# TensorE's order written out by hand in the prompt attention of a hybrid decoder trunk, and the token gates in two passes instead of three

## Chip, cores and metric

One core of one Trainium2 chip runs the whole step. The metric is the device time of one execution in microseconds. Three runs of the kernel before took 1816.46, 1821.41 and 1823.29 us; the median is 1821.41 us.

## What is computed

The reference is one decoder layer on 1024 prompt tokens (`x_prompt`) and 8 x 4 sample tokens (`x_sample`, at positions behind a paged cache of 2048). All is float32. Cut to what matters here:

```python
z = rms_norm(x, g_norm1) @ w_in          # u, v, q, six k/v heads, 24 token gates, 2048 merge gates
o_a = gmlp_mix(gelu(u), layer_norm(gelu(v)))          # mixer A, chunks of 128 tokens
# mixer B: per query head, three attention branches on the same tokens
o_c = softmax(q_n @ kc.T + m_c) @ vc     # compressed blocks (compress() of raw k, v)
o_s = softmax(q_r @ ks.T + m_s) @ vs     # selected blocks of 64 (prompt: 16 of 16, so all are taken)
o_w = softmax(q_r @ kw.T + m_w) @ vw     # sliding window of 512
o_b = g[0] * o_c + g[1] * o_s + g[2] * o_w            # g = sigmoid(token gates)
x = x + (sigmoid(g_a) * (o_a @ w_a) + sigmoid(g_b) * (o_b @ w_b)) @ w_out
x = x + square(relu(rms_norm(x) @ w_up)) @ w_down
```

`compress(rows, w1, w2, pe)` maps every 32 cached k (or v) rows, at a stride of 16, through a small two-layer network. It runs on the prompt's rows and on the 8 samples' caches, for k and for v.

## The kernel before

Products that need float32 precision are made of three products of rounded parts: a value is split into a high part (ScalarE copies it to float32r) and a low part (VectorE or GpSimd subtracts), and TensorE adds high x high, high x low and low x high in PSUM. The helpers are short, so their lines stand for many operations: `cp` (L54, ScalarE copy), `tt` (L57, VectorE with two tensors), `mm` (L73, TensorE matmul), `Weights.split` (L120, the low part of a weight block on VectorE or GpSimd).

The program is unrolled. It is written with a planner: each engine's instructions are ordered ahead of time by a simulated timeline, in which an instruction that comes earlier in the program text, or stands in a `high_priority` block, goes first among those that are ready. A region `tc.manual_schedule(engines={...})` takes the named engines out of the planner's hands: inside it they issue in the order of the program text. The other engines, and instructions outside the region, are still planned. At run time every engine takes its instructions strictly in the order so fixed, and waits on semaphores.

The stages, with their place in the profiled execution: projections of k, v and the token gates (to about 110 us), mixer A and the q projection (to about 233 us), **the prompt's attention** with the samples' compression and twelve merge-gate blocks (about 230 to 705 us), the samples' attention with eight more gate and u blocks (to about 895 us), branch and output projections and the MLP (to the end).

The prompt's attention takes 32 pairs (`pairs`: 8 blocks of 128 queries, each for 4 pairs of heads). A pair's key blocks (selected branch, window branch, one block of compressed keys) are cut into chunks of four blocks of 128 keys: 2 to 7 chunks a pair, 160 in all, 560 blocks. For each chunk there are three pieces:

- an A step (`a_steps`, `step`): `logits` makes the chunk's products of queries and keys on TensorE (bank tag `S`, 3 buffers; tile `P`, 8 buffers); `stat` on VectorE takes row maxima; when all of a head's branch is there, `group` has ScalarE take exponentials, `fin` on VectorE the factors, `scale` on GpSimd multiplies `P`;
- `T(c)`: TensorE transposes the chunk's four blocks of `P` into a bank `PT` (2 buffers); ScalarE copies the high part to `PH`, VectorE subtracts the low part;
- `PV(c)`: TensorE multiplies the values with both parts of `PH` into the pair's bank `O` (1 buffer).

After a pair's last `PV` follows `E`, which adds up, and stores to `o_d`. `q_trans(i)` transposes a pair's queries. In the text before, a pair's `T` runs two chunks ahead of its `PV` (`PV(c)`, then `T(c + 2)`), with A steps of the next pair between them, and the planner may move other work in between on TensorE.

The samples' compression takes 16 blocks (8 samples, k and v): 16 page loads on SP's queue (`raw`, 2 buffers), four quarter splits (`hl`, 2 buffers; ScalarE, then GpSimd or VectorE), 24 matmuls of 256 columns into the single bank `F`, then a small network (`comp_hidden`, `comp_out`, `comp_knorm`) through the same bank. The twelve gate blocks (`fillers` over `W0`) take 72 matmuls of 352 columns each into the single bank `G`; a block's weights (`wraw`, `whl`, one buffer each) are loaded on GpSimd's queue and split by ScalarE and GpSimd, and `gate_evac3` evicts. Compression and gate blocks stand behind the attention in the text, so the planner puts their TensorE work where the attention leaves room.

The token gates (`gates`) are 72 matmuls: 8 k-slices x 3 products x 3 column thirds, with 24 output rows.

Of the kernel before, what the change touches and what calls it, by code (L numbers as in the profile page):

```python
# [15 lines left out]
TB = 352  # L16
# [16 lines left out]
HPU = 2  # L33
# [3 lines left out]
LEAD = 1  # L37
# [8 lines left out]
def build(tc, a):  # L46
# [18 lines left out]
    def mul(out, x, y):  # L65
        return tt(out, x, y, OP.mult)
# [227 lines left out]
    wg = pv.tile([128, 2, 8, 24], F32R, name="wg")  # L294
# [178 lines left out]
    split(wg[:, 0], wg[:, 1], wg_r)  # L473
# [234 lines left out]
    def a_steps(u):  # L708
# [124 lines left out]
    def c_steps(u, chunks, Ps):  # L833
# [32 lines left out]
        def E():  # L866
# [9 lines left out]
            SP.dma_start(o_d[4 + pr, :, qb * 128:(qb + 1) * 128], o)  # L876
# [3 lines left out]
    hp = tc.high_priority()  # L880
    hp.__enter__()
    q_load(0)
    q_load(1)
    q_trans(0)
    prev = None
    for u in range(len(pairs) + 1):
        if u == HPU:
            hp.__exit__(None, None, None)
        A, C = [], 0
        if prev:  # L890
            pu, pch, pPs = prev
            T, PV, E = c_steps(pu, pch, pPs)
            C = len(pch)
            T(0)
            T(1)
        if u < len(pairs):
            chunks, Ps, A = a_steps(u)
            prev = (u, chunks, Ps)
            A.pop(0)()
            q_trans(u + 1)  # L900
        n_a = len(A)
        for c in range(C):
            PV(c)
            T(c + 2)
            k = min(n_a, -(-n_a * (c + LEAD) // C))
            while A and n_a - len(A) < k:
                A.pop(0)()
        while A:
            A.pop(0)()
        if C:  # L910
            E()


# [48 lines left out]
    ctxm = tc.manual_schedule(engines={mybir.EngineType.SP})  # L962
    ctxm.__enter__()
    for which in range(2):
        w1, bias, w2 = c_weights(which)
        for b in range(8):
            raw = cl()
            tg = "FG"[b % 2] if which * 8 + b < N3 else "F"
            pb = bank(tg, 1, psS)
            out = pb[:, 0:256].rearrange("p (k g r) -> p k g r", k=2, r=8)  # L970
            for qt in range(4):
                hl = pa.tile([128, 2, 16, 32], F32R, name="hl", bufs=HIB)
                cols = slice(qt * 32, (qt + 1) * 32)
                with tc.high_priority():
                    cp(hl[:, 0], raw[:, :, cols])
                    (POOL if qt else DVE).tensor_tensor(hl[:, 1], raw[:, :, cols], f(hl[:, 0]), op=OP.subtract)
                hv, lv = (hl[:, i].rearrange("p g (o k r) -> p o k g r", k=2, r=8) for i in range(2))
                for o in range(2):
                    mm(out, w1[:, 0, qt * 2 + o], hv[:, o], qt + o == 0, False)
                    mm(out, w1[:, 1, qt * 2 + o], hv[:, o], False, False)  # L980
                    mm(out, w1[:, 0, qt * 2 + o], lv[:, o], False, qt == 3 and o == 1)
            with tc.high_priority():
                g = comp_hidden(pb[:, 0:256].rearrange("p (k c) -> p k c", k=2), 128, bias, pa)
                pb2 = bank(tg, 1, psS)
                comp_out(pb2[:, 0:128], g, w2)
                if which == 0:
                    z = comp_knorm(pb2[:, 0:128], pa, gkc, 1)
                    pt = bank(tg, 1, psS)
                    PE.transpose(pt[:, 0:128], z, ident)
                    pb2 = pt  # L990
                co = small([128, 128], "co", 1, p=pa)
                cp(co, pb2[:, 0:128])
                POOL.dma_start(c_d[which, b], co)
# [10 lines left out]

    TAGS = {"S": SB, "F": FB, "G": 1}

    def fillers(W, blocks, tag):
        n = 0
        for b in blocks:
            w = W.get(FM_MG + b)  # L1010
            evac = gate_evac3 if b < 16 else u_evac
            for c in range(3):
                cs = slice(c * TB, (c + 1) * TB)
                tg = tag(n)
                n += 1
                ps = bank(tg, TAGS[tg], psS)
                for k in range(8):
                    mm(ps[:, 0:TB], w[:, 0, k], X[:, 0, k, cs], k == 0, False)
                    mm(ps[:, 0:TB], w[:, 0, k], X[:, 1, k, cs], False, False)
                    mm(ps[:, 0:TB], w[:, 1, k], X[:, 0, k, cs], False, k == 7)  # L1020
                with tc.high_priority():
                    evac(b, c, cs, ps)
            W.ahead()

    def fill(W, blocks, tag):

        for b in blocks:
            w = W.get(FM_MG + b)
            for c in range(3):
                cs = slice(c * TB, (c + 1) * TB)  # L1030
                ps = bank(tag, 1, psS)
                for k in range(8):
                    mm(ps[:, 0:TB], w[:, 0, k], X[:, 0, k, cs], k == 0, False)
                    mm(ps[:, 0:TB], w[:, 0, k], X[:, 1, k, cs], False, False)
                    mm(ps[:, 0:TB], w[:, 1, k], X[:, 0, k, cs], False, k == 7)
                with tc.high_priority():
                    (gate_evac3 if b < 16 else u_evac)(b, c, cs, ps)
                if c == 2:
                    W.ahead()
                yield  # L1040

    def gate_evac3(b, c, cs, ps):
        zt = wst0.tile([128, TB], F32, name="zt", bufs=2) if b < NF0 else fp.tile([128, TB], F32, name="yt", bufs=2)
        mul(zt, ps[:, 0:TB], rep[:, cs])
        ACT.activation(zt, zt, AF.Tanh, scale=0.5)
        (ACT if b < 8 else POOL).dma_start(th_d[b, :, cs], zt)

    def u_evac(b, c, cs, ps):
        s_ = fp.tile([128, TB], F32, name="sl", bufs=2)
        POOL.dma_start(s_, s_d[b - 16, :, cs])  # L1050
        zt = fp.tile([128, TB], F32, name="zu", bufs=2)
        mul(zt, ps[:, 0:TB], rep[:, cs])
        y = fp.tile([128, TB], F32, name="yt", bufs=2)
        ACT.activation(y, zt, AF.Square, scale=GC)
        DVE.scalar_tensor_tensor(y, y, 1.0, zt, op0=OP.add, op1=OP.mult)
# [153 lines left out]
    for G in range(2):  # L1209
# [8 lines left out]
        for c in range(5):  # L1218
# [4 lines left out]
            for _ in range(NF1):  # L1223
                next(f1, None)
# [332 lines left out]
```

## Time and profile before

| what | value |
|---|---|
| median of three runs | 1821.41 us |
| profiled execution: its time / its span | 1822.3 us / 1820.5 us |
| instructions | 30327 |
| TensorE matmul busy | 1755.1 us, 96% of the span, 11095 matmuls |
| VectorE / ScalarE / GpSimd busy | 939.4 / 701.3 / 411.3 us |
| mean granted TensorE clock | 0.985 |

The span reaches from the first to the last instruction; 1.8 us of the execution lie outside it. A matmul's busy time includes its modelled way through the array, so that matmuls overlap; what one costs in a stream is read from start to start. [...] PE is TensorE, PEld its weight loads, DVE VectorE, ACT ScalarE, POOL GpSimd, SP the queue that issues most transfers.

### The profile page before, as it was taken

To read this page: it belongs to the slowest core of one execution; us is meant where nothing else is said; L and a number is where in the kernel's file an instruction comes from. 1 tells how busy PE (TensorE), PEld (TensorE's weight loads), DVE (VectorE), ACT (ScalarE), POOL (GpSimd) and SP (SyncE) were. 2 spreads that over 40 slices of the span, in tenths; PEclk is the share of its full clock that TensorE was granted. 3 is DMA by queue.
4 is the path that set the end of the run, shared out by engine and by line. 5 is a ranking of instruction groups with operands and counts; after the bars stand their busy time and mean duration, and the time that the engine had idled before them with its cause. 6 is when DMAs were issued, how large, how long until landed. Compare 5 with 4: busy or idle time off the path is not lost.

```text
span 1820.5 us, 30327 instructions
## 1 busy us (share of the span) xinstructions
PE 1755.1 (96%) x11095; PEld 1657.1 (91%) x11095; DVE 939.4 (52%) x2371; ACT 701.3 (39%) x1681; POOL 411.3 (23%) x603
## 2 busy tenths in 40 slices
PE   8999989999999987999999999999999999999999
PEld 7877878999999975667899999999999999999999
DVE  7637867877777884125664454333333333333333
ACT  5534567777677773222422333201320122003300
POOL 3103465765556653122000220000000000000000
PEclk9999989999999997999899999999999999999999
DMA  5232454333332324666543221111111111111121
GB/s 201 93 99 64 133 152 115 110 102 95 110 95 82 84 63 136 198 195 195 167 154 111 90 75 47 47 47 47 40 43 47 47 47 47 47 47 47 47 83 60
DMA packets 157703, 168.71 MB, mean 93 GB/s; under 512 B 51825, under 2 KB 132338, under 8 KB 157554
## 3 DMA queue, kind: packets, MB, share of 16 engines
q1 hardware_dynamic: 140194, 135.77, 24.0%
q0 software_dynamic: 6464, 20.19, 3.3%
q10 hardware_dynamic: 10896, 10.82, 1.8%
q8 instruction: 87, 1.43, 0.3%
q14 instruction: 62, 0.51, 0.1%
HBM read 136.54 MB, written 29.13 MB: 91 GB/s over the span
## 4 chain that ended last, share of the span: by engine, by line
PE 83%; DVE 7%; DMA 3%; SPq 3%; issue 2%; ACT 2%; POOL 1%; ACTq 0%; DVEq 0%; POOLq 0%
PE S L73 27%; PE G L73 18%; PE PT L73 14%; PE F L73 10%; PE O L73 10%; PE PT L846 2%; SPq L934 2%; DMA ol<-o_d 1%; DVE PH L57 1%; SPq L926 1%; DVE S L776 1%; PE PT L701 1%; DMA ring<-cs 1%; DMA xr<-xT 0%; DMA kct<-c_d 0%
## 5 line engine op out<-in xcount | busy, mean ns | idle before, releaser
L73 PE MATMUL G<-big,whl 128*128 128x352 f32 x1440 | 271.1, 333 | 14.6 <-ACT whl L54 7.6
L73 PEld LDWEIGHTS G<-big,whl 128*128 128x128 f32 x1440 | 235.7, 192 | 43.0 <-issue 17.2
L54 ACT ACTIVATE whl<-wraw 128x1024 fp32r<-128x1024 f32 x100 | 106.1, 1061 | 429.8 <-PE S L73 145.4
L73 PE MATMUL S<-U,whl 128*128 128x352 f32 x864 | 201.0, 323 | 0.0
L73 PE MATMUL S<-H,whl 128*128 128x352 f32 x840 | 189.8, 323 | 0.0
L73 PE MATMUL PT<-U,whl 128*128 128x352 f32 x576 | 154.4, 323 | 0.0
L800 POOL TENSOR_SCALAR P<-P,rs 128x128 f32<-128x128 f32 (+4 forms) x272 | 132.1, 501 | 79.9 <-DVE rs L57 53.0
L73 PEld LDWEIGHTS S<-U,whl 128*128 128x128 f32 x864 | 149.8, 188 | 0.0
L73 PEld LDWEIGHTS S<-H,whl 128*128 128x128 f32 x840 | 144.7, 188 | 0.0
L73 PE MATMUL PT<-H,whl 128*128 128x352 f32 x528 | 142.8, 323 | 0.0
L785 ACT ACTIVATE P<-S,nm 128x512 f32<-128x512 f32 (+3 forms) x208 | 108.8, 532 | 23.2 <-DVE nm L57 14.9
L73 PE MATMUL S<-wt,big 128*128 128x512 f32 x408 | 104.2, 402 | 10.0 <-ACT wt L54 6.4
L57 DVE TENSOR_TENSOR PH<-PT,PH 128x512 fp32r<-128x512 f32 (+2 forms) x160 | 98.5, 618 | 29.4 <-ACT PH L54 28.8
L120 DVE TENSOR_TENSOR whl<-wraw,whl 128x1024 fp32r<-128x1024 f32 x80 | 97.8, 1222 | 15.0 <-ACT whl L54 15.0
L73 PEld LDWEIGHTS PT<-U,whl 128*128 128x128 f32 x576 | 103.2, 188 | 0.0
L73 PE MATMUL O<-PH,V 128*128 128x256 f32 x528 | 95.9, 305 | 6.8 <-DVE PH L57 6.7
L54 ACT ACTIVATE PH<-PT 128x512 fp32r<-128x512 f32 (+2 forms) x160 | 86.6, 544 | 39.0 <-PE PT L846 38.0
L73 PEld LDWEIGHTS S<-wt,big 128*128 128x128 f32 x408 | 76.1, 191 | 27.2 <-ACT wt L54 6.4
L73 PE MATMUL F<-H,whl 128*128 128x352 f32 x312 | 100.9, 323 | 0.0
L73 PE MATMUL S<-KT,QT 128*128 128x128 f32 (+3 forms) x416 | 96.5, 344 | 3.9 <-ACT P L785 2.9
L73 PE MATMUL O<-H,whl 128*128 128x352 f32 x312 | 98.8, 323 | 0.0
L846 PE MATMUL PT<-ident,P 128*128 128x128 f32 x560 | 93.0, 282 | 5.3 <-POOL P L800 3.1
(371 smaller groups left out, 3763.0 us busy)
## 6 DMA issues: line engine op xcount, KB each, us to landing
wraw<-wfm SPq DMA_DIRECT2D x80, 512.0 KB, 3.2
ring<-cs SPq DMA_DIRECT2D x128, 128.0 KB, 2.2
wraw<-wfm POOLq DMA_DIRECT2D x20, 512.0 KB, 4.4
tg<-th_d SPq DMA_DIRECT2D x48, 176.0 KB, 3.0
qdl<-qd_d SPq DMA_DIRECT2D x64, 128.0 KB, 2.8
raw<-cck SPq DMA_DIRECT2D x128, 64.0 KB, 1.9
raw<-ccv SPq DMA_DIRECT2D x128, 64.0 KB, 1.9
wtr<-wtok SPq DMA_DIRECT2D x24, 256.0 KB, 2.6
```

The source lines that it names most:

```text
L54: return ACT.activation(out, in_, AF.Copy, scale=scale)
L57: return DVE.tensor_tensor(out, x, y, op=op)
L73: return PE.matmul(out, l, r, start=start, stop=stop, skip_group_check=skip)
L120: (POOL if i < FM_BR else DVE).tensor_tensor(t[:, 1], raw, f(t[:, 0]), op=OP.subtract)
L701: PE.transpose(pt[:, j], src[:, j], ident)
L776: DVE.tensor_tensor_reduce(S, S, m, scale=-1.0, scalar=3e38, op0=OP.add, op1=OP.min, accum_out=dst)
L785: ACT.activation(Ps[c][:, lo:hi], Ss[c][:, lo:hi], AF.Exp, bias=nm[:, 0, k:k + 1], scale=todo[h, br, i], accum_out=sm[:, i, k:k + 1])
L800: POOL.tensor_scalar(P, P, rs[:, 1, k:k + 1], 1.0, op0=OP.mult, op1=OP.mult)
L846: PE.transpose(pt[:, j], Ps[c][:, j * 128:(j + 1) * 128], ident)
L926: _, vals = nc.values_load_multi_w_load_instructions(ptab[0:1, i0:i0 + 16], engines=[mybir.EngineType.SP], min_val=0, max_val=159, skip_ru ...
L934: SP.dma_start(dst, src)
```

## The change

1. **Token gates.** The high and low weight parts stand side by side in one stationary operand of 56 columns (0 to 23 and 32 to 55, the rest set to zero by GpSimd). Each of 8 k-slices takes 2 products x 3 thirds: 48 matmuls. Behind them, for each third, ScalarE copies the low rows out of PSUM and VectorE adds them to the high rows.
2. **Order by hand.** The attention, the compression and the twelve gate blocks are one `manual_schedule` region for SP and PE. The 160 chunks are steps. In step s TensorE gets, in this order: `PV` of chunk s - 7, the logits of chunk s, at a fixed rate a piece of compression (64 pieces over 166 steps) and a half third of a gate block (72 over 166, 12 matmuls each), once a pair the next queries' transposes, and `T` of chunk s - 6 (`LAG = 6`).
3. **What goes with it.** `compression` and `fill` are generators that yield between pieces; the small tiles `nm`, `sm`, `rs` get 5 buffers; the store of `o_d` moves from SP's queue to GpSimd's; the samples' attention takes twice as many, half as long filler pieces.

```diff
-    wg = pv.tile([128, 2, 8, 24], F32R, name="wg")
+    wg = pv.tile([128, 8, 56], F32R, name="wg")
...
-            for i, j in ((0, 0), (0, 1), (1, 0)):
+            for j in range(2):
                 for c in range(3):
-                    mm(pss[c][0:24, 0:TB], wg[:, i, k], X[:, j, k, c * TB:(c + 1) * TB], k + i + j == 0, k == 7 and i == 1)
+                    mm(pss[c][0:56, 0:TB], wg[:, k], X[:, j, k, c * TB:(c + 1) * TB], k + j == 0, k == 7 and j == 1)
...
-            mul(gt[:, cs], pss[c][0:24, 0:TB], rep[0:24, cs])
+            cp(gt[:, cs], pss[c][32:56, 0:TB])
+            add(gt[:, cs], pss[c][0:24, 0:TB], gt[:, cs])
+            mul(gt[:, cs], gt[:, cs], rep[0:24, cs])
...
-    split(wg[:, 0], wg[:, 1], wg_r)
+    POOL.memset(f(wg), 0.0)
+    split(wg[:, :, 0:24], wg[:, :, 32:56], wg_r)
...
-        nm = small([128, 3, 6], "nm", 3, p=p2)
-        sm = small([128, 3, 6], "sm", 3, p=p2)
-        rs = small([128, 2, 6], "rs", 3, p=p2)
+        nm = small([128, 3, 6], "nm", 5, p=p2)
+        sm = small([128, 3, 6], "sm", 5, p=p2)
+        rs = small([128, 2, 6], "rs", 5, p=p2)
...
-            SP.dma_start(o_d[4 + pr, :, qb * 128:(qb + 1) * 128], o)
+            POOL.dma_start(o_d[4 + pr, :, qb * 128:(qb + 1) * 128], o)
...
-        for c in range(C):
-            PV(c)
-            T(c + 2)
-            k = min(n_a, -(-n_a * (c + LEAD) // C))
-            while A and n_a - len(A) < k:
-                A.pop(0)()
...
-    ctxm = tc.manual_schedule(engines={mybir.EngineType.SP})
...
+    f0, comp = fill(W0, range(NF0), "G"), compression()
+
+    ctxm = tc.manual_schedule(engines={mybir.EngineType.SP, mybir.EngineType.PE})
+    ctxm.__enter__()
+    q_load(0)
+    q_load(1)
+    q_trans(0)
+    A, C, steps = {}, {}, []
+    for u, (qb, pr) in enumerate(pairs):
+        n = -(-(2 * (qb + 1 + min(qb + 1, 5)) + 1) // 4)
+        steps += [(u, c, c == n - 1) for c in range(n)]
+    nc_ = nf_ = 0
+    total = len(steps) + LAG
+    for s_ in range(total + 1):
+        if s_ > LAG:
+            u, c, last = steps[s_ - LAG - 1]
+            C[u][1](c)
+            if last:
+                C.pop(u)[2]()
+        if s_ < len(steps):
+            u, c, last = steps[s_]
+            if c == 0:
+                chunks, Ps, A[u] = a_steps(u)
+                assert len(chunks) == sum(x[0] == u for x in steps)
+                C[u] = c_steps(u, chunks, Ps)
+            A[u][c]()
+        while nc_ * total < 64 * s_:
+            next(comp, None)
+            nc_ += 1
+        while nf_ * total < 6 * NF0 * s_:
+            next(f0, None)
+            nf_ += 1
+        if s_ < len(steps) and steps[s_][1] == 0:
+            q_trans(steps[s_][0] + 1)
+        if LAG <= s_ < total:
+            u, c, last = steps[s_ - LAG]
+            C[u][0](c)
+    for g in (f0, comp):
+        for _ in g:
+            pass
+    ctxm.__exit__(None, None, None)
```

`c_steps` returns `T, PV, E`, so that `C[u][0]` is `T`, `C[u][1]` is `PV` and `C[u][2]` is `E`. `fill` yields after k-slice 3 and after each third; `compression` yields after its second quarter, after its fourth, after `comp_out` and at the block's end.

## Rows read from the trace of the kernel before

**Rows 1.** The page: busy time of TensorE, its share of the span, instructions.

```profile
PE 1755.1 (96%) x11095; PEld 1657.1 (91%) x11095; DVE 939.4 (52%) x2371; ACT 701.3 (39%) x1681; POOL 411.3 (23%) x603
```

**Rows 2.** Windows (us from the start), each engine's busy us, clock, DMA.

```profile
core 0: us, PE busy (x) PEld busy (x) DVE busy (x) ACT busy (x) POOL busy (x), PEclk, DMA share, GB/s
230.00:705.00 475.00, 443.24 (x3140) 423.28 (x3139) 362.61 (x1207) 338.50 (x1001) 282.33 (x467) 0.96 0.33 97
300.00:440.00 140.00, 140.00 (x1025) 137.31 (x1024) 107.50 (x366) 106.63 (x313) 91.77 (x144) 1.00 0.36 104
680.00:716.00 36.00, 24.95 (x151) 21.09 (x151) 20.82 (x63) 14.92 (x43) 15.72 (x22) 0.72 0.29 91
1215.00:1260.00 45.00, 45.00 (x280) 45.00 (x279) 15.01 (x27) 4.25 (x4) 0.00 (x0) 1.00 0.13 43
```

**Rows 3.** Groups by line and tile: count, busy us, mean ns, idle before.

```profile
L73 PE MATMUL S<-KT,QT 128*128 128x128 f32 (+3 forms) x416 | 96.5, 344 | 3.9 <-ACT P L785 2.9 <-DVE nm L57 0.7 <-DVE QT L57 0.3
L73 PE MATMUL O<-PH,V 128*128 128x256 f32 x528 | 95.9, 305 | 6.8 <-DVE PH L57 6.7
L846 PE MATMUL PT<-ident,P 128*128 128x128 f32 x560 | 93.0, 282 | 5.3 <-POOL P L800 3.1 <-DVE QT L57 1.8
L73 PE MATMUL F<-hl,w1s 128*128 128x256 f32 x384 | 61.5, 290 | 0.4 <-ACT co L54 0.4
L993 POOL DMA_DIRECT2D c_d<-co x16 | 9.5, 596 | 8.7 <-ACT co L54 8.7
```

**Rows 4.** TensorE's timeline in the dense part: start, us, what.

```profile
347.97 1.58 PE L73 MATMUL F<-hl,w1s 128*128 128x256 f32 x12
349.39 0.63 PE L73 MATMUL S<-KT,QT 128*128 128x512 f32 x2
349.86 0.64 PE L73 MATMUL O<-PH,V 128*128 128x256 f32 x4
350.33 0.60 PE L846 MATMUL PT<-ident,P 128*128 128x128 f32 x4
350.69 0.56 PE L73 MATMUL G<-big,whl 128*128 128x352 f32 x2
```

**Rows 5.** Timeline near the attention's end, one chunk from T to PV.

```profile
700.66 1.06 PE L846 MATMUL PT<-ident,P 128*128 128x128 f32 x4
...
701.81 0.60 ACT L54 ACTIVATE PH<-PT 128x512 fp32r<-128x512 f32 x1 [2.07 <-PE PT L846]
...
702.44 0.69 DVE L57 TENSOR_TENSOR PH<-PT,PH 128x512 fp32r<-128x512 f32 x1 [1.98 <-ACT PH L54]
...
703.19 1.22 PE L73 MATMUL O<-PH,V 128*128 128x256 f32 x4
```

**Rows 6.** Windows of 4 us around three idle times: PE busy, clock.

```profile
456.00:460.00 4.00, 2.35 (x16) 0.97 0.37 103
460.00:464.00 4.00, 4.00 (x24) 0.60 0.45 150
552.00:556.00 4.00, 2.44 (x12) 0.92 0.27 83
556.00:560.00 4.00, 4.00 (x19) 0.65 0.31 115
664.00:668.00 4.00, 2.46 (x20) 1.00 1.04 315
668.00:672.00 4.00, 3.48 (x30) 1.00 0.09 31
```

**Rows 7.** TensorE's timeline: what stood behind these idle times, in brackets.

```profile
458.27 0.33 PE L989 MATMUL F<-ident,ck_z 128*128 128x128 f32 x1 [1.28 <-DVE ck_z L470]
...
554.04 1.40 PE L73 MATMUL S<-KT,QT 128*128 128x384 f32 x6 [1.56 <-ACT P L785]
...
668.40 0.42 PE L73 MATMUL F<-kct,qp 128*32 128x128 f32 x8 [1.94 <-DMA kct<-c_d]
```

**Rows 8.** Tile hl: min, median, max ns, first and last start us.

```profile
L73 PE MATMUL F<-hl,w1s x384: 272/282/415, 266.1 to 649.2; 128*128 128x256 f32 x192
```

**Rows 9.** Tile wg, the same columns.

```profile
L73 PE MATMUL PT<-big,wg x48: 317/322/406, 93.8 to 106.1; 128*24 128x352 f32 x48
```

**Rows 10.** Tile smask (the samples' ranking), the same columns.

```profile
L1150 DVE TENSOR_SCALAR smask<-cnt x2: 169/171/173, 688.2 to 696.8; 128x30 f32<-128x30 f32 x2
```

More of the change, by code (lines that the diff above doesn't have):

```diff
@@ L36 @@
 N3 = 0
-LEAD = 1
+LAG = 6
 PB = 8
@@ L875, in E, with fill @@
                 POOL.tensor_tensor(o[64 * h:64 * h + 64], t1[0:64, h], t3[:, h], op=OP.add)
-            SP.dma_start(o_d[4 + pr, :, qb * 128:(qb + 1) * 128], o)
+            POOL.dma_start(o_d[4 + pr, :, qb * 128:(qb + 1) * 128], o)
         return T, PV, E
[L880 to L898, printed above, removed]
-            A.pop(0)()
-            q_trans(u + 1)
-        n_a = len(A)
-        for c in range(C):
-            PV(c)
-            T(c + 2)
-            k = min(n_a, -(-n_a * (c + LEAD) // C))
-            while A and n_a - len(A) < k:
[L907 to L911, printed above, removed]
+    def fill(W, blocks, tag):
+        for b in blocks:
+            w = W.get(FM_MG + b)
+            for c in range(3):
+                cs = slice(c * TB, (c + 1) * TB)
+                ps = bank(tag, 1, psS)
+                for k in range(8):
+                    mm(ps[:, 0:TB], w[:, 0, k], X[:, 0, k, cs], k == 0, False)
+                    mm(ps[:, 0:TB], w[:, 0, k], X[:, 1, k, cs], False, False)
+                    mm(ps[:, 0:TB], w[:, 1, k], X[:, 0, k, cs], False, k == 7)
+                    if k == 3:
+                        yield
+                with tc.high_priority():
+                    (gate_evac3 if b < 16 else u_evac)(b, c, cs, ps)
+                if c == 2:
+                    W.ahead()
+                yield
@@ L961, in build @@
     cl = Ahead([lambda w=w, b=b: c_load(w, b) for w in range(2) for b in range(8)], RAWA)
-    ctxm = tc.manual_schedule(engines={mybir.EngineType.SP})
-    ctxm.__enter__()
[L964 to L993, printed above, removed]
@@ new lines, in compression @@
+    def compression():
+        for which in range(2):
+            w1, bias, w2 = c_weights(which)
+            for b in range(8):
+                raw = cl()
+                pb = bank("F", 1, psS)
+                out = pb[:, 0:256].rearrange("p (k g r) -> p k g r", k=2, r=8)
+                for qt in range(4):
+                    hl = pa.tile([128, 2, 16, 32], F32R, name="hl", bufs=HIB)
+                    cols = slice(qt * 32, (qt + 1) * 32)
+                    with tc.high_priority():
+                        cp(hl[:, 0], raw[:, :, cols])
+                        (POOL if qt else DVE).tensor_tensor(hl[:, 1], raw[:, :, cols], f(hl[:, 0]), op=OP.subtract)
+                    hv, lv = (hl[:, i].rearrange("p g (o k r) -> p o k g r", k=2, r=8) for i in range(2))
+                    for o in range(2):
+                        mm(out, w1[:, 0, qt * 2 + o], hv[:, o], qt + o == 0, False)
+                        mm(out, w1[:, 1, qt * 2 + o], hv[:, o], False, False)
+                        mm(out, w1[:, 0, qt * 2 + o], lv[:, o], False, qt == 3 and o == 1)
+                    if qt == 1:
+                        yield
+                yield
+                with tc.high_priority():
+                    g = comp_hidden(pb[:, 0:256].rearrange("p (k c) -> p k c", k=2), 128, bias, pa)
+                    pb2 = bank("F", 1, psS)
+                    comp_out(pb2[:, 0:128], g, w2)
+                yield
+                with tc.high_priority():
+                    if which == 0:
+                        z = comp_knorm(pb2[:, 0:128], pa, gkc, 1)
+                        pt = bank("F", 1, psS)
+                        PE.transpose(pt[:, 0:128], z, ident)
+                        pb2 = pt
+                    co = small([128, 128], "co", 1, p=pa)
+                    cp(co, pb2[:, 0:128])
+                    POOL.dma_start(c_d[which, b], co)
+                yield
@@ L1002, in build @@
     fp = pool("fp")
[L1005 to L1055, printed above, removed]
-        ACT.activation(y, y, AF.Tanh, scale=GT)
-        DVE.scalar_tensor_tensor(y, y, 1.0, zt, op0=OP.add, op1=OP.mult)
-        DVE.scalar_tensor_tensor(y, y, 0.5, s_, op0=OP.mult, op1=OP.mult)
-        POOL.dma_start(o_d[b - 16, :, cs], y)
@@ L1061, in build @@
-    W0 = Weights(wst0, 1, range(FM_MG, FM_MG + NF0))
-    fillers(W0, range(NF0), lambda i: "G")
     ps3 = pool("ps3")
@@ L1222, in build @@
             s_logits(S, qp, G, lambda j: kv[:, :, j, 0:128])
-            for _ in range(NF1):
+            for _ in range(2 * NF1):
                 next(f1, None)
```

18 lines of the change are left out of this document (added).

## The prediction

> **What bounds the kernel now.** I read the page's busy times first. TensorE is busy for 96% of the span [rows 1], so at first sight it bounds everything. But that figure holds the matmuls' way through the array, so the next view is the windows [rows 2]. In an MLP stretch TensorE issues 280 matmuls of 352 columns in 45 us, 0.161 us each, and nothing stands between them: this is what a saturated TensorE looks like. The first 140 us of the dense part of the attention are saturated too, at clock 1.00. The stage as a whole is not: it takes 475 us, and VectorE, the next engine, is busy for 363 of them.
>
> How much TensorE work is in the stage? Counts come from the groups [rows 3] and from the code, prices from start to start in the dense part [rows 4]:
>
> - gate blocks: 12 x 72 = 864 at 0.161 = 139 us;
> - compression: 384 at (349.39 - 347.97)/12 = 0.118, 45 us, and some 40 small ones at about 0.1, 4 us;
> - `PV`: 528, and 64 on compressed keys (two a pair), at (350.33 - 349.86)/4 = 0.118, 70 us;
> - transposes: 560 of `P`, 128 of queries (four a pair), at (350.69 - 350.33)/4 = 0.09, 62 us;
> - logits: 416, and 128 on compressed keys (four a pair). 528 key blocks of 128 columns, each against two query parts, and 128 times 64 columns make 263 columns on average, between 128 (0.09) and 512 (0.235): 0.14 by width, 77 us.
>
> Together 397 us, 2.5 us a step for 160 steps. An upper bound is the mean of the dense part, 140/1025 = 0.137 us, for these 3112: 425 us, but that part holds more of the wide gate matmuls. So 475 - 397 = 78 us are lost to idle time and to a lower clock, much of it at the end, where the windows show TensorE busy for 25 of 36 us at a mean clock of 0.72. These 78 us are the most that a better order can win.
>
> **The order by hand.** The matmuls stay the same; their order and their waits change. I follow TensorE through one step: `PV(s-7)`, logits of s, a piece of compression, a half third of a gate block, `T(s-6)`. Then the next step begins, and it begins with `PV(s-6)`. Between `T` of a chunk and `PV` of the same chunk stands nothing. LAG gives the softmax six steps, but the way from the transposes through ScalarE's high part and VectorE's low part back to TensorE gets no cover at all, and TensorE cannot take anything else, since its order is fixed. The queue behind the waiting `PV` is everything: the next logits, and so VectorE's row maxima and ScalarE's exponentials; compression; gate blocks. Before, `T` ran two chunks ahead of its `PV`, with logits and other work between.
>
> The price is in the trace where nothing else is left to cover it, near the attention's end [rows 5]. The four transposes end at 701.72, ScalarE's copy takes 0.60, VectorE's subtraction 0.69, and `PV` starts at 703.19: 1.47 us. From start to start it is more: four transposes fill 0.36 us of TensorE, but end 0.60 after their start [rows 4], so the loss is 1.47 + 0.24 = 1.71 us. Of the 160 chunks 32, each pair's last, have one to three blocks and cost less; 1.6 us is my mean and my lower bound. On top comes waiting in the queues of ScalarE and VectorE: each step has on average 338/160 = 2.1 us of ScalarE work and 363/160 = 2.3 us of VectorE work [rows 2], and the exponentials of the step's own logits become ready at about the time that the transposes end. Nothing excludes a wait of one full exponential; nothing in steps with few fillers forces any. I bound it by 0 and 0.9 us and take 0.35, nearer to the lower end because both engines would be less than half busy in longer steps. So each step loses 1.95 us, and 160 steps lose 312 us.
>
> **The clock.** An idle time of 1.28 us in a dense stretch [rows 7] was followed by 4 us at a mean clock of 0.60, and one of 1.56 us by 0.65; one of 1.94 us was followed by 1.00 [rows 6]. So waits of this size often, not always, put TensorE back to half speed for a while. Here there is one every step. The nearest stretch is the attention's end: 25 of 36 us busy, clock 0.72 [rows 2]. In the new steps the fillers make longer busy runs, so I take 0.8 for the stage; the ends are 1.00 and 0.50. At 0.8 the 397 us become 496.
>
> [...]
>
> **Where the stage starts and ends.** In step 1 the first piece of compression stands in TensorE's order. Its first matmul came at 266 before [rows 8], bound by page loads that cannot begin sooner, and I keep that. Before, attention and gate matmuls ran ahead of it; now nearly all wait behind it. So the stage ends at 266 + 496 + 312 = 1074 us instead of 705: +369. The samples' ranking, ready at 697 before [rows 10] and so hidden under the attention, needs memory and the bank `F` that compression now holds to the last step; the gate fillers cover most of that chain, I add 8 us, between 0 and the 29 us from the first product on the samples' compressed keys at 668 [rows 7] to the ranking's end.
>
> **What costs nothing.** 32 stores of `o_d` move to GpSimd's queue; a like one there takes 0.596 us [rows 3], 19 us on an engine busy for 282 of 475 us, in a stage that gets longer: the cover is its own idle time. Were that gone, `P` would come later, with six steps of slack behind it. On SP only loads are left, in text order: page loads can hold up a pair's query load, which has a pair's length to spare. The larger buffers of `nm`, `sm` and `rs` are needed since six steps can span four pairs. A gate block's split (ScalarE, then GpSimd) has over two steps until the next block's first matmul, some 10 us. VectorE's work of 2.3 us a step stays below the step.
>
> **The gates.** 24 of 72 matmuls go. They stood among 12.3 us [rows 9], so at most 24 x 0.17 = 4 us; the added copies and additions lengthen a chain that q and v matmuls cover; if not covered, they could eat the gain. I take -3, between -4 and 0.
>
> **Sum.** The profiled execution took 1822.3 us with a span of 1820.5, 0.9 above the median of the three runs. 1822.3 + 369 + 8 - 3 = 2196 us. Everything behind the stage moves back unchanged.
>
> **The rivals.**
>
> - *The clock stays up* (25%). Same waits, but the idle times are too short to lower the clock: 266 + 397 + 312 = 975, +270, with the other terms 2097 us. With no queueing, 160 x 1.6 = 256 us, it is 2041. For it: the 1.94 us idle time without a fall. Against it: the two others, and a wait in every step.
> - *The clock stays down* (12%). All matmuls at half speed, 794 us, and 1.8 us a step because slower TensorE leaves emptier queues: 266 + 794 + 288 = 1348, +643, 2470 us. Against it: runs of compression and gate matmuls let it recover, as the dense part shows.
> - *Not slower* (4%). The copy and the subtraction would have to be hidden so far that a step loses under (705 - 266 - 397)/160 = 0.26 us, which decides the sign; with none the stage ends at 663 and the time is 1822.3 - 42 + 5 = 1785 us. For it: the lost 78 us exist, and gate work would be left for the end. Against it: [rows 5] alone, over six times that per step.
> - The forecast has 55%; 4% remain for a mishap that I don't see, such as queueing far above 0.9 us.
>
> **Range.** From 2050 (clock up, nearly no queueing) to 2380 (clock near 0.62: 640 us, and 2.2 us a step: 266 + 640 + 352 = 1258, +553). It holds the forecast, most of the second case and little of the third, some 8 in 10. Faster by over 0.5% (the least that tells from no change here, some 9 us): 0.04; within 0.5%: 0.01; slower: 0.95.
>
> **What the profile would show.** Right: `PV` matmuls waiting on VectorE's `PH` about 160 times, 250 to 400 us in all, where now 6.8 us stand [rows 3]; a period of 4.5 to 6 us from one logits group to the next; granted clock between 0.6 and 0.9 through the stage; gate matmuls to its very end; the stage ending near 1070; 48 gate matmuls. Wrong: if `PV` waits stay below 1 us a step, if another wait (a bank `S`, weights of a gate block, pages) is larger than that on `PH`, or if the MLP changes too.

## The result and the profile after

The changed kernel takes 2156.69 us (median of four runs, 2153.15 to 2162.02) against 1820.99 us of the kernel before on the same chip: 1.185 times as long, with a 95% interval of 1.183 to 1.187. The forecast was 2196 us with a range of 2050 to 2380. The profiled execution of the changed kernel took 2157.89 us with a span of 2156.1 us, that of before 1822.3 us.

The page of the changed kernel: first TensorE's and the other engines' busy times, then two lines of the 40 slices, then the group of the `PV` matmuls.

```profile
PE 1842.8 (85%) x11071; PEld 1715.0 (80%) x11071; DVE 969.1 (45%) x2374; ACT 717.6 (33%) x1684; POOL 428.7 (20%) x636
...
PE   8999567666666666666799899999999999999999
...
PEclk9999788889988899898899999999999999999999
...
L73 PE MATMUL O<-PH,V 128*128 128x256 f32 x528 | 105.8, 324 | 222.4 <-DVE PH L57 222.4
```

Against [rows 1] TensorE has 24 instructions fewer, is busy for 88 us longer and fills 85% of the span instead of 96%. The slices say where: from the fifth to the twentieth, 54 us each, it is busy for five to seven tenths at a granted clock of seven to nine tenths, and after that it is full as before. The `PV` group waits 222 us on VectorE's low part, where [rows 3] had 6.8.

Next the waits of TensorE over the attention stage, 255 to 1038 us: what was waited for, total us, times, the longest.

```profile
PE O L73 <- DVE PH L57: 251.5, 159, 3.6
PE F L73 <- ACT hl L54: 21.1, 1, 21.1
```

One wait has taken the stage over: 159 of the 160 chunks wait, for 251.5/159 = 1.58 us each (the 64 `PV` matmuls on compressed keys are included here, which the page's group leaves out). The second line, 21 us once, ends where the first compression matmul begins; the stage's other two waits, not shown, come to 1.3 us. The tiles of the stage's start and end, and of the ranking behind it (min, median, max ns, first and last start):

```profile
L73 PE MATMUL F<-hl,w1s x384: 272/286/581, 255.3 to 1011.6; 128*128 128x256 f32 x192
...
L73 PE MATMUL O<-PH,V2C x64: 274/386/583, 278.3 to 1037.0; 128*128 128x256 f32 x64
...
L1144 DVE TENSOR_SCALAR smask<-cnt x2: 165/173/181, 1045.0 to 1053.2; 128x30 f32<-128x30 f32 x2
```

Compression begins at 255.3, where [rows 8] had 266.1, and the last `PV` stands at 1037.0, where the kernel before had 705.2. Medians tell of the clock too: the `PV` on compressed keys has 386 ns in the middle of its 64, before it had 283. Two of them took 0.80 us at 444.06, at a granted clock of 0.50, and in the kernel before 0.40 at 342.35, at 1.00.

TensorE's timeline of two steps (start, us, what, the idle time before it in brackets):

```profile
432.19 0.60 PE L849 MATMUL PT<-ident,P 128*128 128x128 f32 x4
432.82 0.60 ACT L54 ACTIVATE PH<-PT 128x512 fp32r<-128x512 f32 x1 [0.16 <-PE PT L849]
433.45 0.69 DVE L57 TENSOR_TENSOR PH<-PT,PH 128x512 fp32r<-128x512 f32 x1 [0.42 <-ACT PH L54]
434.20 0.75 PE L73 MATMUL O<-PH,V 128*128 128x256 f32 x4 [1.41 <-DVE PH L57]
434.78 0.53 PE L73 MATMUL S<-KTC,QT 128*128 128x64 f32 x4
435.14 2.18 PE L73 MATMUL G<-big,whl 128*128 128x352 f32 x12
437.16 0.60 PE L849 MATMUL PT<-ident,P 128*128 128x128 f32 x4
437.36 1.06 ACT L54 ACTIVATE whl<-wraw 128x1024 fp32r<-128x1024 f32 x1 [0.52 <-PE G L73]
438.32 0.58 ACT L54 ACTIVATE PH<-PT 128x512 fp32r<-128x512 f32 x1
438.93 0.69 DVE L57 TENSOR_TENSOR PH<-PT,PH 128x512 fp32r<-128x512 f32 x1 [1.05 <-ACT PH L54]
439.68 0.74 PE L73 MATMUL O<-PH,V 128*128 128x256 f32 x4 [1.92 <-DVE PH L57]
```

The first step shows the bare way: transposes end at 432.79, copy and subtraction follow with 0.03 us between them, and TensorE has stood still for 1.41 us. In the second step ScalarE is still splitting a gate block's weights (`whl`, 1.06 us) when the transposes end at 437.76, so the copy begins 0.56 us behind them instead of 0.03, and TensorE waits 1.92 us. This is the queueing for which the prediction took 0.35 us a step.

### The profile page after: what moved, and what is told of

It is laid out like the page before. It is cut to its first block, busy times and chain, and to the rows that moved or that the text cites. A ratio compares the mean times of both kernels' runs of the same rounds, so it can differ in the third digit from the quotient of the medians.

```text
span 2156.1 us, 30189 instructions
## 1 busy us (share of the span) xinstructions
PE 1842.8 (85%) x11071; PEld 1715.0 (80%) x11071; DVE 969.1 (45%) x2374; ACT 717.6 (33%) x1684; POOL 428.7 (20%) x636
## 4 chain that ended last, share of the span: by engine, by line
PE 76%; DVE 9%; ACT 8%; issue 3%; SPq 2%; DMA 2%; POOL 0%; ACTq 0%; DVEq 0%; POOLq 0%
PE S L73 25%; PE G L73 17%; PE PT L73 12%; PE O L73 11%; PE F L73 9%; DVE PH L57 4%; ACT PH L54 3%; PE PT L849 2%; ACT P L788 2%; SPq L942 1%; ACT hl L54 1%; DMA ol<-o_d 1%; DVE S L779 1%; DVE QT L57 1%; SPq L934 1%
## 5 line engine op out<-in xcount | busy, mean ns | idle before, releaser
L73 PE MATMUL G<-big,whl 128*128 128x352 f32 x1440 | 291.3, 358 | 6.1 <-DVE zu L57 4.5
L73 PE MATMUL O<-PH,V 128*128 128x256 f32 x528 | 105.8, 324 | 222.4 <-DVE PH L57 222.4
L73 PEld LDWEIGHTS G<-big,whl 128*128 128x128 f32 x1440 | 267.2, 216 | 35.0 <-issue 16.5
L73 PEld LDWEIGHTS O<-PH,V 128*128 128x128 f32 x528 | 76.4, 202 | 256.2 <-DVE PH L57 256.0
L779 DVE CUSTOM_DVE_ANT_0 S<-S,mask 128x256 f32<-128x256 f32 (+3 forms) x160 | 77.1, 482 | 131.1 <-PE S L73 126.5
L73 PE MATMUL S<-wt,big 128*128 128x512 f32 x408 | 107.3, 411 | 10.6 <-ACT wt L54 6.6
```

The lines of the kernel that those rows point to most:

```text
L73: return PE.matmul(out, l, r, start=start, stop=stop, skip_group_check=skip)
L779: DVE.tensor_tensor_reduce(S, S, m, scale=-1.0, scalar=3e38, op0=OP.add, op1=OP.min, accum_out=dst)
```

## Experiments

All times stand beside runs of the kernel before on the same chip. Each edit is against the changed kernel unless another is named.

| run | median us | ratio to before, 95% |
|---|---|---|
| the change | 2156.69 | 1.185 (1.183 to 1.187) |
| e1_pv_late | 1901.73 | 1.044 (1.040 to 1.048) |
| e2_gates_only | 1820.18 | 0.9997 (0.9984 to 1.0010) |
| e3_text_planned | 1851.36 | 1.017 (1.013 to 1.020) |
| e4_fill_behind_t | 1988.18 | 1.094 (1.091 to 1.098) |
| e5_high_only | 2001.34 | 1.100 (1.096 to 1.104) |
| e6_late_start | 1905.49 | 1.047 (1.045 to 1.049) |
| e7_pv_later | 1893.71 | 1.040 (1.038 to 1.042) |
| e8_logits_first | 1893.28 | 1.040 (1.038 to 1.042) |
| e9_planned_lead | 1819.20 | 0.9989 (0.9979 to 0.9998) |
| e10_fine_pieces | 1899.40 | 1.043 (1.041 to 1.045) |
| e11_spread_planned | 1813.01 | 0.995 (0.994 to 0.997) |

**`PV` one step later (e1).** A whole step of other matmuls now stands between `T` and the `PV` of the same chunk.

```diff
-    for s_ in range(total + 1):
-        if s_ > LAG:
-            u, c, last = steps[s_ - LAG - 1]
+    for s_ in range(total + 2):
+        if s_ > LAG + 1:
+            u, c, last = steps[s_ - LAG - 2]
```

> The changed kernel with one index moved: PV of a chunk stands a whole step behind its T, with the next logits, compression and gate work between them; all else, the order by hand too, stays. Theory (the uncovered way from T to PV, and the clock that it pulls down, are the whole loss): waits of PV on PH fall from 252 us to under 25 us, the granted clock of the stage is above 0.95, the attention ends between 660 and 690 us, and the time is 1775 to 1800 us, below the kernel before. Rival (a fixed order on TensorE is what costs, whichever wait shows it): another wait of 100 us or more takes its place and the time stays above 1950 us.

It measured 1901.73 us: 255 us of the 336 are back, the rest is not. TensorE's waits over its stage:

```profile
PE F L73 <- ACT hl L54: 21.6, 1, 21.6
PE O L73 <- DVE PH L57: 20.7, 26, 3.6
PE O L73 <- DVE o_t L57: 15.5, 16, 1.5
PE PT L849 <- DVE QT L57: 5.7, 8, 2.1
PE S L73 <- ACT P L788: 5.2, 4, 1.9
PE G L73 <- POOL whl L120: 5.1, 5, 2.2
```

The wait on `PH` fell from 251.5 us in 159 times to 20.7 in 26, and others came up in its place: on `o_t`, which frees the accumulator `O`; on the transposed queries; on exponentials; on a gate block's low part. So the placement of `PV` right behind `T` is the main cause, shown by one edit, but my expectation that the kernel would then be faster than before missed by 100 us: an order by hand has a second cost.

**The gates alone (e2).** Against the kernel before: `wg` with the low part in rows 32 to 55, two passes, copy and addition behind them, and nothing else of the change.

```diff
-            for i, j in ((0, 0), (0, 1), (1, 0)):
+            for j in range(2):
...
-                    mm(pss[c][0:24, 0:TB], wg[:, i, k], X[:, j, k, c * TB:(c + 1) * TB], k + i + j == 0, k == 7 and i == 1)
+                    mm(pss[c][0:56, 0:TB], wg[:, k], X[:, j, k, c * TB:(c + 1) * TB], k + j == 0, k == 7 and j == 1)
```

> The kernel before with the token gates alone in two passes of 56 columns. Theory: 24 matmuls fewer at 0.17 us, so 1 to 4 us faster, ratio 0.998 to 1.000, with 48 matmuls on the gate weights. Rival: the three added copies and additions lengthen the chain to the sigmoid, and the time rises by 1 to 3 us.

1820.18 us over 12 runs, a ratio of 0.9997: between 3 us saved and 2 us lost. The gates' tile shows the matmuls gone:

```profile
L73 PE MATMUL PT<-big,wg x32: 317/321/405, 94.0 to 102.2; 128*56 128x352 f32 x32
```

They end 3.9 us earlier than in [rows 9], as I had counted, and in the profiled execution the attention's last `PV` is earlier too, 702.1 instead of 705.2. The medians differ by 0.9 us, and their interval holds both the 3 us that I had forecast and none: whether the gain reaches the end of the kernel is not shown.

**The changed text, TensorE's order planned (e3).** The steps, the spreading and the text's order stay; only SP's order is fixed, as it was before.

```diff
-    ctxm = tc.manual_schedule(engines={mybir.EngineType.SP, mybir.EngineType.PE})
+    ctxm = tc.manual_schedule(engines={mybir.EngineType.SP})
```

> The changed kernel's text with TensorE given back to the planner (SP alone stays by hand). Theory: the planner puts other ready work between T and PV, so PV waits on PH stay under 60 us and the time is 1790 to 1850 us. Rival (the text itself costs: LAG of 6, the finer pieces, o_d on GpSimd's queue, more buffers): the time stays above 2000 us with TensorE planned.

1851.36 us, 305 us of the 336 back. The planner moves other matmuls into the gap between `T` and `PV`; the wait that the text would cause is nearly gone:

```profile
PE O L73 <- DVE PH L57: 11.9, 19, 1.8
```

It is still 32 us slower than before. The order of the text, even where it only guides the planner, costs something too: e9 below keeps the finer pieces, the larger buffers and the stores on GpSimd's queue, has another order, and does not lose these 32 us.

**Fillers behind `T` (e4).** Query transposes and `T` go ahead of compression and gate pieces, so that in a step with a filler this covers the chain.

```diff
+        if s_ < len(steps) and steps[s_][1] == 0:
+            q_trans(steps[s_][0] + 1)
+        if LAG <= s_ < total:
+            u, c, last = steps[s_ - LAG]
+            C[u][0](c)
         while nc_ * total < 64 * s_:
...
-        if s_ < len(steps) and steps[s_][1] == 0:
-            q_trans(steps[s_][0] + 1)
-        if LAG <= s_ < total:
-            u, c, last = steps[s_ - LAG]
-            C[u][0](c)
```

> The changed kernel with T moved ahead of compression and gate work within its step, so that the step's filler, where it has one, covers the way from T to PV. Pieces: 64 of compression and 72 of gates over 166 steps, so some two thirds of the steps have some cover, mostly 1.4 to 1.9 us. Theory: PV waits on PH fall from 252 us to 90 to 140 us, the clock of the stage rises from 0.88 to above 0.9, time 1940 to 2020 us. Rival (fixed order): little change, above 2100 us.

1988.18 us, half of the loss. The 72 gate pieces and 64 compression pieces cover about half of the chunks:

```profile
PE O L73 <- DVE PH L57: 128.3, 85, 3.3
```

Those left wait nearly as long as in the change, 1.51 us each. The window of its stage (window, us, busy times, then granted clock):

```profile
266.00:855.00 589.00, 455.04 (x3038) 420.72 (x3036) 363.21 (x1154) 338.19 (x975) 286.04 (x486) 0.95 0.23 68
```

With half as many waits the clock rises from 0.89 to 0.95. From the change to e4 the waits on `PH` fall by 123 us and the time lost to the clock by 85 - 29 = 56 us (11% of 771 us, 5% of 589, both estimates from above, since some of the slow time falls into waits), together 179. The two profiled executions differ by 2157.89 - 1975.29 = 183 us, the medians by 168: e4's profiled execution is the shortest of its five.

**A shorter chain (e5).** `PV` reads the high part twice, and so waits for ScalarE's copy alone; the kernel leaves out the low part's product.

```diff
-                    mm(O[:, h], v.rearrange("p a d -> p (a d)"), ph[:, :, j], c == 0 and j == 0, False, True)
+                    mm(O[:, h], v.rearrange("p a d -> p (a d)"), ph[:, 0:1, j].to_broadcast([128, 2, 128]), c == 0 and j == 0, False, True)
...
-                        mm(O[:, h], V2C[:, h, kv].rearrange("p a d -> p (a d)"), ph[:, :, j], False, True, True)
+                        mm(O[:, h], V2C[:, h, kv].rearrange("p a d -> p (a d)"), ph[:, 0:1, j].to_broadcast([128, 2, 128]), False, True, True)
```

> The changed kernel with PV reading the high part of PH twice in place of the high and the low part, so that it waits for ScalarE's copy but not for VectorE's subtraction, which still runs; TensorE's work is the same. It leaves the low part's product out of the attention's output. Theory: the waits fall by 0.6 to 0.85 us in each of 160 steps, from 252 us to 115 to 160 us. If the clock goes by how long the waits are, it rises to above 0.92 and the time is 1950 to 2000 us; if it goes by how many there are, it stays near 0.88 and the time is 2010 to 2060 us. Rival (fixed order): above 2100 us.

2001.34 us. The number of waits stays, their length falls by VectorE's 0.67 us:

```profile
PE O L73 <- ACT PH L54: 144.4, 158, 2.7
```

```profile
266.00:881.00 615.00, 469.18 (x3051) 420.96 (x3049) 357.71 (x1161) 341.22 (x981) 288.50 (x486) 0.96 0.22 65
```

That is 0.91 us each and 107 us less in all, and the clock stands at 0.96: 25 us lost instead of 85, by the same estimate. 107 + 60 = 167 us; the profiled executions differ by 159, the medians by 155. So the chain's two parts can be told apart, and both the wait and the clock follow its length: the number of waits stayed, and the clock rose all the same.

**What else the order by hand costs (e6, e7, e8, e10).** Four tries, the first on e1 and each on the one before: compression starts eight steps and gate pieces three steps into the stage (e6); `PV` lags one step more (e7); the step's logits go ahead of `PV` (e8); gate blocks in pieces of six matmuls instead of twelve, at twice the rate (e10, on e8).

```diff
-        while nc_ * total < 64 * s_:
+        while s_ > 8 and nc_ * (total - 8) < 64 * (s_ - 8):
...
-        while nf_ * total < 6 * NF0 * s_:
+        while s_ > 3 and nf_ * (total - 3) < 6 * NF0 * (s_ - 3):
```

> The kernel with PV a step later (first experiment), and compression starting at step 9, gate work at step 4, both spread evenly over what is left. It asks what the wait of 21.6 us for the first split of the compression's pages costs. Theory: TensorE does the first logits and gate work in that time, the wait falls under 6 us, the attention ends 12 to 20 us earlier (758 to 766) and the time is 1880 to 1890 us. Rival: the same work is only crowded into later steps, whose other waits grow: 1897 us or more.

e6 measured 1905.49 us, no gain over e1 where I had expected 12 to 20 us. The wait for the first `hl` fell from 21.6 to 12.2 us, and others, on query copies (9.2 instead of 5.7) and on the first gate block's high part (8.2 us, once, before the first compression matmul), made up for it.

```diff
-        if s_ > LAG + 1:
-            u, c, last = steps[s_ - LAG - 2]
+        if s_ > LAG + 2:
+            u, c, last = steps[s_ - LAG - 3]
```

> As the late start, and PV one more step behind T (two whole steps). It asks whether the waits of PV on PH that were left with one step between (20.7 us on matmuls, 30.3 on weight loads) are from too little lead. Theory: they fall under 8 us and the time falls by another 15 to 30 us, to 1850 to 1875 us. Rival (VectorE's order is what holds PH, and it moves along): waits on PH or on others stay, less than 8 us gained.

e7 measured 1893.71 us, 12 us less than e6 and short of the 15 to 30 that I had expected. No `PV` waits on `PH` any more; instead TensorE waits on `o_t` (16.7 us), exponentials (11.0) and query copies (10.6).

```diff
-        if s_ > LAG + 2:
-            u, c, last = steps[s_ - LAG - 3]
...
         if s_ < len(steps):
             u, c, last = steps[s_]
...
             A[u][c]()
+        if s_ > LAG + 2:
+            u, c, last = steps[s_ - LAG - 3]
...
```

> As the one before, with the next logits ahead of PV in the step, so that a pair's last sums (o_t, from the only bank O) have the logits' time before the next pair's first PV, and the row maxima start earlier. Theory: the waits of PV on o_t (15.5 us on matmuls, 16 times, with PV first) fall under 5 us, and the time falls by 8 to 20 us against the run before. Rival: PV first had been hiding the logits' wait for a bank S, and logits now wait for ScalarE's exponentials by as much.

e8 measured 1893.28 us, the same: the waits on `o_t` fell from 16.7 to 9.9 us, not under 5, and others grew. Its longest waits from 255 us on:

```profile
PE PT L849 <- DVE QT L57: 14.3, 8, 2.8
PE F L73 <- ACT hl L54: 11.8, 1, 11.8
PE F L73 <- DVE ch_g L454: 10.8, 8, 3.1
PE O L73 <- DVE o_t L57: 9.9, 10, 2.0
PE PT L849 <- DVE PH L57: 6.1, 8, 1.5
PE S L73 <- ACT P L788: 5.2, 6, 2.0
```

No line leads; one more, 8.2 us on the first gate block's weights, stands before 255. Each is a product that comes late in some steps only: the queries of a new pair, the compression's activation, the accumulator at a pair's end, a bank still being read.

```diff
-                    if k == 3:
+                    if k in (1, 3, 5):
                         yield
...
-        while s_ > 3 and nf_ * (total - 3) < 6 * NF0 * (s_ - 3):
+        while s_ > 3 and nf_ * (total - 3) < 12 * NF0 * (s_ - 3):
...
-            for _ in range(2 * NF1):
+            for _ in range(4 * NF1):
```

> By hand again, logits first and PV two steps behind T, with gate pieces of 6 matmuls in place of 12, twice as many. It asks whether the coarse pieces (1.9 us in 43% of the steps, nothing in the others) cause the small waits that are left. Theory of coarse pieces: steps get more alike, and the time falls by 15 us or more, under 1878. Rival (bursts on VectorE and ScalarE at a pair's last chunks, bank O and QT, set them): within 10 us of 1893.

e10 measured 1899.40 us: finer pieces bring nothing, and ten waits of 18.9 us in all on a gate block's low part appear.

**The same text, planned (e9).** Against e8, with TensorE's order again left to the planner.

```diff
-    ctxm = tc.manual_schedule(engines={mybir.EngineType.SP, mybir.EngineType.PE})
+    ctxm = tc.manual_schedule(engines={mybir.EngineType.SP})
```

> The text of the run with logits first and PV two steps behind T (1893 us by hand), with TensorE given back to the planner. Theory (with the lead repaired, what is left of the loss is the fixed order's own: work that is ready cannot pass work that waits): the planned version takes 1835 to 1860 us, 35 to 60 us less than by hand. Rival (the even spread in the text is what costs): it stays within 15 us of 1893.

1819.20 us, 74 us less than e8 with the same text. The window of each one's stage, first e8, then e9:

```profile
266.00:766.00 500.00, 432.38 (x2996) 412.56 (x2993) 343.61 (x1104) 328.12 (x934) 282.72 (x471) 0.95 0.28 82
```

```profile
266.00:696.00 430.00, 407.61 (x2983) 389.73 (x2982) 335.07 (x1081) 312.55 (x922) 278.55 (x458) 1.00 0.32 94
```

And the waits of e9, its three longest:

```profile
PE PT L849 <- DVE PH L57: 8.2, 12, 2.2
PE PT L849 <- DVE QT L57: 3.0, 2, 1.6
PE S L73 <- ACT P L788: 1.4, 3, 0.7
```

In the planned order another matmul stands wherever one of these products is late: query copies cost 3.0 us instead of 14.3, and the clock stays at 1.00. Of e8's 70 us in the window, 45 are idle time of TensorE (500 - 432.4 against 430 - 407.6), and about 500 x 0.05 = 25 are clock. This edit shows the second cost of the order by hand, 74 us. Leaving one engine to the planner lets it order the other engines' work to match, though, so how much is TensorE's order itself and how much is ScalarE's and VectorE's was not told apart. The text's order matters even when planned: from e3 to e9 the time falls by 32 us, by the later `PV`, the logits ahead of it and the later start of compression and gates together; which of them does it was not told apart.

**Spreading alone (e11).** The kernel before with its own attention loop and planned order; only the twelve gate blocks are taken out of their place behind it and emitted evenly over the chunks.

```diff
+    f0, nf_, ns_ = fill(W0, range(NF0), "G"), 0, 0
...
+            ns_ += 1
+            while u >= HPU and nf_ * 160 < 3 * NF0 * ns_:
+                next(f0)
+                nf_ += 1
...
-    fillers(W0, range(NF0), lambda i: "G")
+    for _ in f0:
+        pass
```

> The kernel before with its own loop and T two chunks ahead of PV, TensorE planned, and only the gate blocks' thirds written into the text among the attention's chunks (36 over 160), so that the planner may not run them all off by 617 us. It asks whether an even spread is worth something by itself. Theory of the change (gate work left for the end fills the idle time of the last 90 us): the attention ends up to 30 us earlier and the time is 1785 to 1812 us. Rival (gate work written early is preferred to later attention and delays it): 1822 us or more.

1813.01 us, a ratio of 0.995 (0.994 to 0.997): the fastest version, 8 us ahead of the kernel before, about the 0.5% that the prediction named as the least that tells. Its last `PV` on compressed keys starts at 681.6, where the kernel before had 705.2:

```profile
L73 PE MATMUL O<-PH,V2C x64: 276/283/415, 234.3 to 681.6; 128*128 128x256 f32 x64
```

Most of these 23 us are given back just behind it (windows as above):

```profile
680.00:700.00 20.00, 14.09 (x75) 12.70 (x74) 3.32 (x9) 5.67 (x14) 10.99 (x19) 0.83 0.84 273
700.00:720.00 20.00, 14.24 (x88) 12.86 (x86) 4.86 (x11) 3.34 (x11) 4.04 (x5) 0.90 0.59 184
```

TensorE is busy for 14 of 20 us in each, while DMA runs at 84% and 59%. The trace shows what came later instead, compression and behind it the samples' ranking:

```profile
L73 PE MATMUL F<-hl,w1s x384: 272/282/393, 265.8 to 681.1; 128*128 128x256 f32 x192
L73 PE MATMUL F<-kct,qp x16: 272/285/298, 703.2 to 711.6; 128*32 128x128 f32 x16
L1156 DVE TENSOR_SCALAR smask<-cnt x2: 172/176/180, 727.6 to 739.1; 128x30 f32<-128x30 f32 x2
```

With gate work spread among the chunks, the last compression matmul stands at 681.1 instead of 649.2 [rows 8], the ranking's first product at 703.2 instead of 668.4 [rows 7], and its last mask at 739.1 instead of 696.8 [rows 10]. So this chain, which ended under the attention before, now stands behind it. I read the lost gain as this; no run tested it.

## Why the prediction was right, and what it missed

**The place.** As forecast, `PV` waits on `PH` in every step, 159 times, and the total of 251.5 us is at the lower end of the 250 to 400 that I gave as the sign. Shown by e1 (a step between `T` and `PV`) and by e5 (a shorter chain).

**The size of a step's loss.** Forecast 1.95 us from start to start; measured 1.58 us of waiting, with the 0.24 of the prediction kept 1.82 us, and 160 x 1.82 = 290 us instead of 312. The bare wait stands at 1.41 us in the timeline after, near the 1.47 of [rows 5]; with my mean of 1.6 us for a step kept, queueing comes to 1.82 - 1.6 = 0.22 us, not 0.35.

**The clock.** Forecast 0.8, with 397 us of work becoming 496. The stage took 1037 - 255 = 782 us; without the 290 us of waits 492 are left for the same work. The window gives the clock directly:

```profile
266.00:1037.00 771.00, 518.30 (x3053) 467.27 (x3051) 365.79 (x1165) 341.90 (x980) 286.67 (x487) 0.89 0.18 52
```

The clock has two levels here: of the 771 windows of 1 us in this stretch 561 show 1.00, 138 show 0.50, 72 a value between and none a lower one (the kernel before, 230 to 705: 431, 29, 15 and none). So a mean of 0.89 is 22% of the time at 0.50, 170 us (174 by the 1 us windows), and costs 11% of 771: at most 85 us, an estimate from the mean, since some of these 170 fall into waits. The two 0.8 and 0.89 are not the same mean, for mine was over the work and this is over the stage with its waits; 397/492 = 0.81 is the one to compare. That it comes so close is partly luck: with my upper bound of 425 us for the work it would be 0.86. The 10 us and more between 492 - 397 = 95 and the clock's 85 are no other waits, of which the stage has 1.3 us; the 397, a count by hand, may be low by that much, and no run shows it. The rival in which the clock stays up is out for the stage: the mean is 0.89, with waits of 1.58 us on average and 3.6 at most. Single waits do leave the clock up, as that of 1.94 us in [rows 7] did, with 1.00 behind it [rows 6]; which ones, no row here says.

**Start and end.** The stage began at 255, 11 us before what I had kept from [rows 8]. My reason, that page loads cannot begin sooner, was wrong: the first began at 242.4 us instead of 248.9, and ScalarE's first split at 254.7 instead of 263.9. The stage ended at 1037 instead of 1074. In all +332 against +369: 11 from the start, 22 from the waits, 4 from the clock.

**Behind the stage.** From the end of the last `PV` to the end of the span there are 2156.1 - 1037.3 = 1118.8 us, before 1820.5 - 705.6 = 1114.9: +4, where I had +8 for the ranking, whose last mask now stands at 1053 and thus behind the stage as expected.

**The gates.** -3 forecast; e2 measured between 3 us saved and 2 lost, which neither bears it out nor excludes it. Whatever it is lies inside the stage's 332, for these are read from the start of the span.

**The sum.** 332 + 4 = 336; the two profiled executions differ by 2157.9 - 1822.3 = 335.6. Of the other signs, a step took 782/160 = 4.9 us, between the 4.5 and 6 that I gave, and the MLP is unchanged: 280 matmuls in the 45 us from 1500 on.

**What the costs at nothing did.** Apart from the 21 us before the first compression matmul, which lie in the start that I kept, no wait on SP's queue, GpSimd's stores or the bank `F` of more than 1.1 us stands beside the one on `PH` in the stage's waits; the covers that I named held.

**What it missed.** I put 1785 us to the rival in which the chain is hidden. The runs in which it is hidden by hand (e1, e6, e7, e8) end between 1893 and 1905: hiding this one chain was not enough, since with TensorE's order fixed the products that are late in some steps were waited for: 14.3 us on query copies in e8, where the planned order of the same text (e9) had 3.0. I had counted one wait per step and no others. That did not touch the forecast, because these waits lay behind the larger one, but its upside was wrong by some 110 us. Part of that was in my 78 us of loss: by [rows 2] TensorE was idle for 475 - 443 = 32 us and lost at most 0.04 x 475 = 19 to the clock, 51 in all, and the fastest version tried (e11) gained 8. What stays open is which of e8's many small waits sets the rest: later start, lag, order within a step and finer pieces each moved waits from one product to another and the time by 12 us at most.

## What to carry to other kernels

When an engine's order is fixed by hand, follow each product from the instruction that starts it to the one that takes it, and put at least the chain's length in other work between them: a lag on the first product of a pipeline (six steps for the softmax) covers nothing of a later chain (transpose, copy, subtraction, product) that is left inside one step. Before fixing the order, run the same text with the planner's order: here that alone told 305 of the 336 us apart, and even the best order by hand stayed 74 us behind the planned one with the same text. And price a wait in a dense TensorE stream with what it does to the clock behind it: here 1.6 us of waiting in each step cost up to another 0.5 us in slower matmuls (85 us over 160 steps).

## What the hardware showed that I had not expected

The time at the granted clock of 0.50 per wait grew steeply from the shorter waits of e5 to the longer ones of the change. Estimated from the mean clocks of the windows above, with the two levels that the change showed, it is 170 us for 159 waits in the change (1.07 us each, at 1.58 us of waiting), 59 us for 85 in e4 (0.69 us, at 1.51 us) and 49 us for 158 in e5 (0.31 us, at 0.91 us), with the rounding of the mean clock worth some 8 us on each total; other idle times are in these totals too. Of the three only e5 stands apart with certainty. e4's trace is that of its shortest run, 1975.29 us at a mean clock of 0.971, and its median run has 1988.18 us at 0.965. Over a whole run that is 2 x 0.035 x 1986.4 - 2 x 0.029 x 1973.5 = 25 us more at 0.50, an estimate from the runs' clocks; if they fall into this stage, e4 has some 84 us, 1.0 us per wait, as the change has at nearly the same length of wait.

How a single step looks at 0.50, in the changed kernel's timeline:

```profile
410.37 1.22 PE L73 MATMUL O<-PH,V 128*128 128x256 f32 x4 [3.63 <-DVE PH L57]
411.38 0.90 PE L73 MATMUL S<-KTC,QT 128*128 128x64 f32 x4
412.09 3.87 PE L73 MATMUL G<-big,whl 128*128 128x352 f32 x12
```

After a wait of 3.63 us the twelve gate matmuls take 3.87 us, at a granted clock of 0.50 from 412 to 416, where the same piece took 2.18 us at 435.14, at 1.00. And how fast the clock comes back (4 us windows of the same kernel: window, us, TensorE's busy us, granted clock, DMA share, GB/s):

```profile
436.00:440.00 4.00, 2.08 (x15) 1.00 0.00 0
440.00:444.00 4.00, 1.99 (x11) 0.59 0.50 157
444.00:448.00 4.00, 3.94 (x18) 0.56 0.70 189
448.00:452.00 4.00, 2.59 (x18) 1.00 0.50 144
```

In windows of 0.5 us it is 1.00 to 440.5, 0.50 from 441.0 to 447.5 and 1.00 from 448.0 to 456. So it fell about 1 us behind the wait of 1.92 us that ended at 439.68, stayed down through that of 2.06 us before 444.06 and 3.4 us of work behind it, and the waits of 1.41 us before 451.77 and 454.82 left it at 1.00 that far. I have no row that says why one wait brings it down and the next doesn't.
